# Index scores over 128 rows in both passes, half of the modulation steps moved into the index loop, and the odd attention's mask as constant rows of queries and keys

## The chip, the cores and the metric

The kernel runs on one core of one Trainium2 chip. The metric is the device time of one execution in microseconds (us), the median of several runs. Five engines work side by side: PE (TensorE, matrix products), DVE (VectorE), ACT (ScalarE), POOL (GpSimd) and SP, whose queue issues nearly all DMAs here. Each works through its own instructions in order.

## The reference, cut to what matters

The reference is a two-layer encoder over 1024 positions of width 1024. Before each sub-layer the stream is modulated by six vectors made from a conditioning vector `c`. Layer 0 picks, for every query, 256 keys by an index score, and layer 1 has a latent attention with a chunk mask:

```python
cond = jax.nn.silu(c)
mod = (cond @ ada_w[l] + ada_b[l])[:, None, :]          # six parts of 1024
sh_m, sc_m, g_m, sh_f, sc_f, g_f = jnp.split(mod, 6, axis=-1)
...
limit = (qpos // 64 + 1) * 64                            # end of the query's own chunk
rel = relu(einsum('bthd,bsd->bths', q_idx, k_idx))       # 8 index heads of 64
score = einsum('bths,bth->bts', rel, w_scaled)           # then top 256 below the limit
...
logits = einsum('bthd,bshd->bhts', qh, kh) * scale       # layer 1: 64 + 32 rotary rows
logits = where(key_pos < limit, logits, NEG); p = softmax(logits)
```

## The kernel before

Everything lies transposed, with channels in the 128 partitions. A product in float32 accuracy is made of passes over a high and a low part: `mm3` (lines 286 to 291) issues three matmuls, at lines 288, 289 and 290.

**Index stage.** `index` (line 1528) runs over blocks of 128 queries from 7 down to 2, and in each over four index heads; it is called for heads 0 to 3 and then for heads 4 to 7, so 48 heads in all. `scores2` makes the scores of one head in chunks of up to 512 keys, each by two matmuls: line 1307 with all 128 rows of the head's query tile (64 rows hold the high part, the other 64 the low part) against `kih`, and line 1308 with the 64 high rows alone against `kil`. ACT takes the relu into `rl` (line 1537), and DVE adds it, weighted, to `dd` (lines 1540 and 1542). PE has two score buffers, and `rl` has two. After each head, 1.4 or 1.6 steps of the projections behind it are put into PE's order; a step is one `mm3` of 512 columns.

**Bisection.** The threshold of each query is found bit by bit, 31 bits from 30 down (lines 1680 to 1700). In a bit DVE proposes a candidate (`cand`, line 1618), ACT counts three blocks by their signs (line 1624), DVE counts three more (line 1576), and DVE decides (lines 1636 and 1637). Between counts and decision stands one `mods.step()`: one of 32 loads of 128x1024 modulation weights, and one DVE product with the conditioning row, summed along the row (line 377). Nine bits in ten also take one half projection, 24 matmuls of 512 columns; every second half projection has its weights divided, high on ACT (line 266) and low on DVE (line 267). DVE's and ACT's order here is that of the code, and PE's order is that of the code everywhere; elsewhere a scheduler orders DVE, ACT and POOL. Then come the exact threshold and the masks on DVE, and PE does what projections are left.

**Odd attention.** 64 units (8 heads, 8 query blocks each) go through a pipeline. `unit` (line 2027) makes scores from rows 0 to 95 of the query and key tiles, and then one matmul of one row and 64 columns (line 2033) adds the mask, a large negative number where the first 64 queries of a block meet the last 64 keys. Key tiles come from a ring of three, query tiles from a ring of two. Ahead of the pipeline stand the keys and queries of head 0 and eight products of values (`uv`), each copied out by ACT (`mv`, line 2067).

Of the kernel before, what the change touches and what calls it, by code (L numbers as in the profile page):

```python
# [10 lines left out]
F32 = mybir.dt.float32  # L11
F32R = mybir.dt.float32r
# [3 lines left out]
ALU = mybir.AluOpType  # L16
# [3 lines left out]
P = 128  # L20
D = 1024
S = 1024
# [12 lines left out]
NEGMASK = -float(2 ** 100)  # L35
# [37 lines left out]
def layout(inp):  # L73

    a = {}
# [95 lines left out]
    f = np.float32  # L171
# [24 lines left out]
    a["c_cnt"] = np.ascontiguousarray(  # L196
        np.broadcast_to((1.0 / cnt).astype(f).reshape(1, 64), (P, 64))
    )
    mk = np.zeros((1, 192), f)
    mk[0, :64] = 1.0  # L200
    mk[0, 128:] = NEGMASK
    a["c_mask"] = mk
    return a


# [1 line left out]
def trunk(ctx, tc, t, out):  # L207
    nc = tc.nc
    V, A, G, T = nc.vector, nc.scalar, nc.gpsimd, nc.tensor

    def pool(name, bufs=1, side="left", space=None):
        if space is not None:
            return tc.tile_pool(name=name, bufs=bufs, space=space, reuse_waits="tile")
        return tc.tile_pool(name=name, bufs=bufs, side=side, reuse_waits="tile")
# [27 lines left out]
    def load(dst, src, eng=None):  # L242
        (eng or nc.sync).dma_start(dst, src)
# [910 lines left out]
    class Unit:  # L1154
# [10 lines left out]
        def scores(self):  # L1165
            n = S if self.i >= 4 else HALF
            self.ps = self.psum.tile([P, n], F32, tag=f"s{n}", name="s", bufs=1)
            self.scores_fn(self.ps)
# [129 lines left out]
            A.copy(dst[n][own, c], src[own])  # L1298
            V.tensor_tensor(dst[n][rest, c], src[own], dst[n][own, c].bitcast(F32), ALU.subtract)

    def scores2(ps, i, q, kh, kl, rows):

        qc = slice(i * P, (i + 1) * P)
        w = (i + 1) * P
        for c in range(0, w, HALF):
            e = min(c + HALF, w)
            T.matmul(ps[:, c:e], lhsT=q[:, qc], rhs=kh[:, c:e], start=True, stop=False)
            T.matmul(ps[:, c:e], lhsT=q[rows, qc], rhs=kl[rows, c:e], start=False, stop=True)
            spend(2 * max(e - c, 256) / 2400.0)


# [15 lines left out]
    tmp = ipx.enter_context(pool("idxtmp", bufs=2, side="right"))  # L1327
    start = ExitStack()
    tmp0 = start.enter_context(pool("start", bufs=3))
    bias0 = bias_of(0, tmp0)  # L1330
    kih = ip.tile([P, S], F32R, name="kih")
    kil = ip.tile([P, S], F32R, name="kil")
    wiT = ip.tile([P, S], F32, name="wiT")
    wi = ip.tile([P, 8, 8], F32, name="wi")
    qi = ip.tile([P, 8, S], F32R, name="qi")
# [44 lines left out]
    for k in range(KD):  # L1380
# [22 lines left out]
    for hf in range(2):  # L1403
        c = half(hf)
        ps = first[0][2][:, c]
# [26 lines left out]
    ps = bank("wit")  # L1432
# [11 lines left out]
    class Projections:  # L1444
# [75 lines left out]
        def taps(self, m):  # L1520
            u, y = self.conv["u"], yb[:, m]
            A.mul(y, u[:, 0:S], ctap[:, m, 0:1])
            for k in (1, 2):
                V.scalar_tensor_tensor(
                    y, u[:, k : k + S], ctap[:, m, k : k + 1], y, ALU.mult, ALU.add
                )

    def index(heads, others, rate):
        n = 0.0
        for i in range(7, 1, -1):  # L1530
            w_ = (i + 1) * P
            for hd in heads:
                rows = slice(64 * (hd % 2), 64 * (hd % 2) + 64)
                ps = bank2("idx_s")
                scores2(ps, i, qi[:, hd], kih, kil, rows)
                rl = tmp.tile([P, S], F32, tag="rl", name="rl")
                A.activation(rl[:, :w_], ps[:, :w_], AF.Relu)
                wc = wi[:, i, hd : hd + 1]
                if hd == 0:
                    V.tensor_scalar(dd[i], rl[:, :w_], wc, None, ALU.mult)  # L1540
                else:
                    V.scalar_tensor_tensor(dd[i], rl[:, :w_], wc, dd[i], ALU.mult, ALU.add)
                n += rate
                while n >= 1.0:
                    next(others, None)
                    n -= 1.0
    products = Projections().steps()
    index(range(4), chain(more_queries(3), products), FILL[0])
    index(range(4, 8), products, FILL[1])
    ipx.close()  # L1550
    yb = evy.enter_context(pool("evyb")).tile([P, 4, S], F32, name="yb")
    evkv = ExitStack()
# [12 lines left out]
    tmp = prj.enter_context(pool("prj", bufs=1, side="right"))  # L1565
    sel = ExitStack()
    tk = sel.enter_context(pool("tk", side="right"))
    eq = tk.tile([P, S], F32, name="eq")
    pre = tk.tile([P, S], F32, name="pre")
    junk = [tk.tile([P, S], BF16, name=f"junk{e}") for e in "va"]  # L1570

    cond_row = bank2("cond_row")
    mods = Modulation(None, tk, 0, range(2, 6), D, 0, cond_row, (eq, pre))

    def count(cnt, d, w, thr, op):
        V.tensor_scalar(junk[0][:, :w], d, thr, 0.0, op, ALU.add, accum_out=cnt)
# [105 lines left out]
    with tc.manual_schedule(engines={E.DVE}):  # L1682
        rows_ = Rows()
        rows_.setup()
        with tc.manual_schedule(engines={E.Activation}):
            pace = 0.0
            for bit in range(30, -1, -1):
                rows_.propose(bit)
                rows_.signs()
                rows_.counts()  # L1690
                mods.step()
                pace += PACE
                if pace >= 1.0:
                    advance()
                    pace -= 1.0
                rows_.decide()
            advance()
            mods.step()
        for nm, src in (("q", q32), ("k", k32)):
            split(*pairs[0, nm], src[:, 0])  # L1700
        rows_.step_up()
        rows_.result()
        rows_.mask()
# [10 lines left out]
    with ExitStack() as s:  # L1714
        pp = s.enter_context(pool("pair", bufs=2, side="right"))
# [107 lines left out]
    odp = od.enter_context(pool("od"))  # L1823
# [5 lines left out]
    load(pws, t["pool_s"])  # L1829
    latg = odp.tile([P, 5], F32, name="latg")  # L1830
    load(latg, t["lat_g"])
    mask = odp.tile([1, 192], F32R, name="mask")
    ones_lat = odp.tile([P, 2, P], F32, name="ones_lat")
    V.memset(ones_lat[:, 0], 1.0 / 384)
    V.memset(ones_lat[:, 1], 1.0 / 256)
# [14 lines left out]

    with ExitStack() as s:
        tmp = s.enter_context(pool("odprj", bufs=1))
        mraw = tmp.tile([1, 192], F32, tag="pu", name="mraw")
        load(mraw, t["c_mask"])
        V.tensor_copy(mask, mraw)
        edge = tmp.tile([P, 4, 16], F32, name="edge")
        V.memset(edge, 0.0)

# [102 lines left out]
    with ExitStack() as s:  # L1961
# [5 lines left out]
        v32 = vp.tile([P, 8, HALF], F32, name="mv32")  # L1967
        kk_, qq_, vv_ = {}, {}, {}

        def prepare_k(m):  # L1970
            kh = [pp.tile([P, S], F32R, tag="kh", name="kh", bufs=3) for _ in range(2)]
            kl = [pp.tile([P, S], F32R, tag="kl", name="kl", bufs=3) for _ in range(2)]
            for e in range(2):
                kk_[2 * m + e] = (kh[e], kl[e])
            raw = fetch(t["w_uk"][m], f"uk{m}")
            yield
            yield
            w = divide(raw, t["w_uk"].shape[-1], f"uk{m}", "pool")
            yield
            for e in range(2):  # L1980
                split(kh[e][64:96], kl[e][64:96], kr[64:96], lo_eng="pool")
            for hf in range(2):
                c = half(hf)
                ps = bank("uk")
                project(ps, w, P, [(a[:, c], b[:, c]) for a, b in kvx])
                yield
                for e in range(2):
                    split(kh[e][0:64, c], kl[e][0:64, c], ps[64 * e : 64 * e + 64])
                    if e == 0:
                        yield  # L1990

        def prepare_q(hd):
            raw = fetch(t["w_uq"][hd], f"uq{hd}")
            qh = pp.tile([P, S], F32R, tag="qh", name="qh")
            ql = pp.tile([P, S], F32R, tag="ql", name="ql")
            qq_[hd] = (qh, ql)
            yield
            yield
            w = divide(raw, t["w_uq"].shape[-1], f"uq{hd}", "pool")
            yield  # L2000
            qts = []
            for hf in range(2):
                c = half(hf)
                ps = bank("uq")
                project(ps, w, P, [(lat[:, 0, k, c], lat[:, 1, k, c]) for k in range(3)])
                yield
                qt = tmp.tile([P, HALF], F32, tag="q32", name="qt")
                A.mul(qt[0:64], ps[0:64], 96 ** -0.5)
                rotate(qt[64:96], ps, 64, 64, c, tmp, "rq1", "rq2")
                qts.append((c, qt))  # L2010
            yield
            for c, qt in qts:
                split(qh[0:96, c], ql[0:96, c], qt[0:96], lo_eng="pool")
                yield
# [10 lines left out]
                pass  # L2025

        def unit(hd, i, first):
            w_ = (i + 1) * P
            m, n = hd // 2, hd % 2

            def sc(ps):
                scores(ps, i, qq_[hd], kk_[hd], slice(0, 96))
                T.matmul(
                    ps[:, w_ - 64 : w_], lhsT=mask[:, 0:128], rhs=mask[:, 128:192],
                    start=False, stop=True, skip_group_check=True,
                )

            def peak(ps, pr, mx):
                V.tensor_reduce(mx, ps, AX.X, ALU.max, negate=True)

# [12 lines left out]

            return Unit(tmp, psum, (2,2), i, first, sc, peak, weigh, lambda: vv_[hd], put, store)
# [92 lines left out]
```

## Time and profile before

| | us |
|---|---|
| median of 3 runs (2680.07 to 2691.18) | 2689.89 |
| profiled execution, device time | 2674.74 |
| span of the profiled execution, first to last instruction | 2672.9 |
| index stage, first score matmul to last `dd` | 82.7 to 199.9 |
| bisection, first candidate to last decision | 211.2 to 388.5 |
| exact threshold and masks on DVE | 388.5 to 459 |
| odd attention, first score on PE to last | 1633.2 to 1843 |

A view by stretches gives each engine's busy time in it; the timeline gives single instructions, with the idle time ahead of them in brackets and what ended it. PEclk 1.00 stands for 2.4 GHz and 0.50 for 1.2 GHz. A matmul's stated duration overlaps the next one, so its price is read from start to start.

### The profile page before, as it was taken

To read this page: it belongs to the slowest core of one execution; us is meant where nothing else is said; L and a number is where in the kernel's file an instruction comes from. 1 tells how busy PE (TensorE), PEld (TensorE's weight loads), DVE (VectorE), ACT (ScalarE), POOL (GpSimd) and SP (SyncE) were. 2 spreads that over 40 slices of the span, in tenths; PEclk is the share of its full clock that TensorE was granted. 3 is DMA by queue.
4 is the path that set the end of the run, shared out by engine and by line. 5 is a ranking of instruction groups with operands and counts; after the bars stand their busy time and mean duration, and the time that the engine had idled before them with its cause. 6 is when DMAs were issued, how large, how long until landed. Compare 5 with 4: busy or idle time off the path is not lost. (4 is left out here: it accounts for less than half of the span.)

```text
span 2672.9 us, 32638 instructions
## 1 busy us (share of the span) xinstructions
PE 2467.4 (92%) x10922; PEld 1936.7 (72%) x10922; DVE 2157.8 (81%) x3491; ACT 1364.8 (51%) x2427; POOL 1054.5 (39%) x800
## 2 busy tenths in 40 slices
PE   6999998999888989998999899999888999998997
PEld 5567776887666767786777677787666888877786
DVE  6549899777698999978887866877698877788977
ACT  3446751765554444554333546766464555563434
POOL 0000001645674222424547634643865333334546
PEclk9899999999989989999999999999989999999999
DMA  6004430013434555335323331123533322244313
GB/s 244 32 18 136 139 118 16 17 68 120 129 104 153 183 173 166 126 98 178 91 75 95 105 101 61 54 75 106 173 100 103 107 86 84 95 128 148 102 47 105
DMA packets 123690, 284.43 MB, mean 106 GB/s; under 512 B 15361, under 2 KB 23042, under 8 KB 122626
## 3 DMA queue, kind: packets, MB, share of 16 engines
q1 hardware_dynamic: 122370, 278.16, 32.8%
q10 hardware_dynamic: 1152, 4.19, 0.4%
q8 instruction: 86, 1.41, 0.2%
q14 instruction: 82, 0.67, 0.1%
HBM read 234.06 MB, written 48.23 MB: 106 GB/s over the span
## 5 line engine op out<-in xcount | busy, mean ns | idle before, releaser
L702 DVE SCALAR_TENSOR_TENSOR cv<-u,taps,cv 128x512 f32<-128x512 f32 x352 | 311.1, 910 | 19.1 <-ACT cv L700 17.5
L267 POOL TENSOR_TENSOR v<-v,v 128x512 fp32r<-128x512 f32 x8 | 12.6, 1580 | 443.6 <-ACT v L266 443.6
L998 DVE SCALAR_TENSOR_TENSOR r<-dn,mod,r 128x512 f32<-128x512 f32 x198 | 147.0, 745 | 44.4 <-PE dn L290 42.5
L833 POOL TENSOR_TENSOR s<-rawg 128x512 f32<-128x512 f32 (+3 forms) x60 | 79.4, 1323 | 256.4 <-DVE wlo_ups L267 87.3
L700 ACT ACTIVATE cv<-u,taps 128x512 f32<-128x512 f32 x176 | 124.3, 721 | 58.0 <-DMA z<-cv 32.8
L288 PE MATMUL up<-t,wh 128*128 128x512 f32 x288 | 119.5, 415 | 33.1 <-ACT u L872 33.1
L706 ACT ACTIVATE cv<-cv 128x512 f32<-128x512 f32 x88 | 55.6, 632 | 144.7 <-DVE cv L702 143.9
L289 PE MATMUL up<-h_f,whi_up 128*128 128x512 f32 x256 | 105.5, 412 | 24.8 <-DVE h_f L267 24.8
L872 ACT COPY u<-up 128x512 f32<-128x512 f32 x144 | 83.9, 583 | 75.8 <-issue 35.3
L267 DVE TENSOR_TENSOR wl<-rawg,wh 128x512 fp32r<-128x512 f32 (+3 forms) x120 | 116.1, 970 | 2.6 <-ACT wh L266 2.4
L289 PE MATMUL up<-t,wh 128*128 128x512 f32 x288 | 117.7, 409 | 0.0
L290 PE MATMUL up<-t,wl 128*128 128x512 f32 x288 | 117.3, 407 | 0.0
L288 PE MATMUL up<-h_f,whi_upa 128*128 128x512 f32 x288 | 114.6, 398 | 1.2 <-ACT whi_upa L266 1.2
L834 POOL TENSOR_TENSOR s<-s,raw_upv 128x512 f32<-128x512 f32 x36 | 51.4, 1428 | 161.9 <-DMA raw_upv<-in_w_up 145.7
L266 ACT CAST wh<-rawg 128x512 fp32r<-128x512 f32 (+3 forms) x120 | 65.0, 545 | 97.6 <-PE dn L289 52.4
L290 PE MATMUL up<-h_f,wlo_upa 128*128 128x512 f32 x288 | 113.7, 395 | 0.7 <-DVE wlo_upa L267 0.7
L267 DVE TENSOR_TENSOR pl<-pt,ph 128x128 fp32r<-128x128 f32 (+2 forms) x192 | 99.4, 546 | 18.3 <-ACT ph L266 18.1
L266 ACT CAST ph<-pt 128x128 fp32r<-128x128 f32 (+2 forms) x192 | 85.3, 480 | 54.6 <-PE pt L1197 53.1
L289 PE MATMUL up<-h_f,whi_upa 128*128 128x512 f32 x288 | 113.0, 392 | 0.0
L290 PE MATMUL up<-h_f,wlo_up 128*128 128x512 f32 x256 | 104.6, 409 | 6.0 <-POOL wlo_up L267 6.0
L288 PE MATMUL up<-h_f,whi_up 128*128 128x512 f32 x256 | 106.4, 416 | 2.9 <-ACT h_f L266 1.9
L1624 ACT ACTIVATE junka<-dd,cand 128x384 bf16<-128x384 f32 (+2 forms) x93 | 87.1, 936 | 39.9 <-DVE cand L1618 37.9
(750 smaller groups left out, 8617.3 us busy)
## 6 DMA issues: line engine op xcount, KB each, us to landing
mod_raw<-in_ada_w SPq DMA_DIRECT2D x96, 256.0 KB, 2.9
z<-cv SPq DMA_DIRECT2D x88, 256.0 KB, 2.0
raw_upv<-in_w_up SPq DMA_DIRECT2D x36, 512.0 KB, 3.7
rawg<-in_w_up SPq DMA_DIRECT2D x34, 512.0 KB, 3.7
raw_up<-in_w_up SPq DMA_DIRECT2D x32, 512.0 KB, 3.7
z<-z SPq DMA_DIRECT2D x56, 256.0 KB, 2.9
xa_dram<-xo SPq DMA_DIRECT2D x48, 256.0 KB, 2.1
raw_dr<-in_w_dr SPq DMA_DIRECT2D x32, 384.0 KB, 3.1
```

Of the source, the lines that this page charges most:

```text
L266: A.copy(hi, src)
L267: (V if lo_eng == "dve" else G).tensor_tensor(lo, src, hi.bitcast(F32), ALU.subtract)
L288: T.matmul(ps, lhsT=wh, rhs=xh, start=start, stop=False, skip_group_check=more)
L289: T.matmul(ps, lhsT=wh, rhs=xl, start=False, stop=False, skip_group_check=more)
L290: T.matmul(ps, lhsT=wl, rhs=xh, start=False, stop=stop, skip_group_check=more)
L700: A.activation(y[n], u[:, 0:HALF], AF.Copy, scale=self.taps[:, c, 0:1])
L702: V.scalar_tensor_tensor(y[n], u[:, k : k + HALF], self.taps[:, c, k : k + 1], y[n], ALU.mult, ALU.add,)
L706: A.activation(y[1], y[1], AF.Silu)
L833: G.tensor_tensor(s1, g[:, c0], g[:, c1], ALU.add)
L872: A.copy(dst, ps)
L998: V.scalar_tensor_tensor(r, ps, self.gate[:, dt : dt + 1], r, ALU.mult, ALU.add)
L1624: A.activation(junk[1][:, :w], d, AF.Sign, bias=self.col(self.cand.bitcast(F32), j), scale=-1.0, accum_out=self.col(self.cnt, j),)
```

## The change

In `scores2` the second pass runs over all 128 rows too. `Modulation` is made twice: parts 2 and 3 (16 steps) with their own buffers inside `index`, a step after every even head of blocks 7 to 3 until 16 are done, and parts 4 and 5 in the bisection, on odd bits and once behind them. In the odd attention the query and key tiles are fixed, two and three pairs, rows 96 to 127 of each are filled once from a table, and the mask matmul goes.

```diff
+    mk = np.zeros((32, 2, 8, 2, 64), f)
+    mk[np.arange(8), 0, np.arange(8), 0] = 1.0
+    mk[np.arange(8), 1, np.arange(8), 1] = NEGMASK
+    a["c_mask"] = mk.reshape(32, 2 * S)
...
-            T.matmul(ps[:, c:e], lhsT=q[rows, qc], rhs=kl[rows, c:e], start=False, stop=True)
+            T.matmul(ps[:, c:e], lhsT=q[:, qc], rhs=kl[:, c:e], start=False, stop=True)
...
+    modx = ExitStack()
+    modp = modx.enter_context(pool("modp"))
+    mods = Modulation(modp, modp, 0, range(2, 4), D, 3)
...
-                scores2(ps, i, qi[:, hd], kih, kil, rows)
+                scores2(ps, i, qi[:, hd], kih, kil)
+                if i > 2 and hd % 2 == 0:
+                    mods.step()
...
-    mods = Modulation(None, tk, 0, range(2, 6), D, 0, cond_row, (eq, pre))
+    mods = Modulation(None, tk, 0, range(4, 6), D, 0, cond_row, (eq, pre))
...
-                mods.step()
+                if bit % 2:
+                    mods.step()
...
+        for n, tiles in enumerate((qtile, ktile)):
+            raw = tmp.tile([P, S], F32, tag="prb", name="mask_raw", bufs=2)
+            load(raw[96:], t["c_mask"][:, n * S : (n + 1) * S])
+            for hi, lo in tiles:
+                A.copy(hi[96:], raw[96:])
+                V.tensor_tensor(lo[96:], raw[96:], hi[96:].bitcast(F32), ALU.subtract)
...
-                scores(ps, i, qq_[hd], kk_[hd], slice(0, 96))
-                T.matmul(
-                    ps[:, w_ - 64 : w_], lhsT=mask[:, 0:128], rhs=mask[:, 128:192],
-                    start=False, stop=True, skip_group_check=True,
-                )
+                scores(ps, i, qq_[hd], kk_[hd], slice(0, P))
```

On DVE, at the start of the index stage, this stood before: `wi` are the head weights, `dd_98` and `dd_97` (`dd7` below) the scores of blocks 7 and 6, and `qi` the rest of the queries.

```order
L1435 COPY wi<-wit 128x64
L1540 TENSOR_SCALAR dd_98<-rl,wi 128x1024
L1542 SCALAR_TENSOR_TENSOR dd_98<-rl,wi,dd_98 128x1024 x3
L1540 TENSOR_SCALAR dd_97<-rl,wi 128x896
L1542 SCALAR_TENSOR_TENSOR dd_97<-rl,wi,dd_97 128x896
L1299 TENSOR_TENSOR qi<-qi 64x512
```

And now from the same copy on (lines are those of the changed kernel; `mod_raw` is a modulation step, whose row sum is the row behind it):

```order
L1436 COPY wi_126<-wit_633 128x64
L378 ISA mod_raw_721,mod_acc_660<-mod_raw_721,cond_row0_652 128x1024
L378 ISA mod_acc_660 128x1
L1547 TENSOR_SCALAR dd7_98<-rl_664,wi_126 128x1024
L378 ISA mod_raw_753,mod_acc_660<-mod_raw_753,cond_row0_652 128x1024
```

The scheduler does not leave the steps behind every second head: two stand ahead of this copy, and all 16 stand before the tenth of the 48 `dd` instructions, with the last casts of `qi` among them.

On PE, the first two units of the odd attention stood so, with the mask matmul at the end of each:

```order
L288 MATMUL s<-kh,qh 128x128
L289 MATMUL s<-kl,qh 128x128
L290 MATMUL s<-kh,ql 128x128
L2033 MATMUL s<-mask 128x64
L288 MATMUL s<-kh,qh 128x512
L289 MATMUL s<-kl,qh 128x512
```

Now the same two units run into each other:

```order
L289 MATMUL s<-kh_12953,qh_12959 128x128
L290 MATMUL s<-kl_12954,qh_12959 128x128
L291 MATMUL s<-kh_12953,ql_12960 128x128
L289 MATMUL s<-kh_12953,qh_12959 128x512
L290 MATMUL s<-kl_12954,qh_12959 128x512
```

64 mask matmuls are gone, and nothing stands in their place.

On ACT, ahead of that pipeline, the copies of the value products (`mv`) were broken only by the query casts. Now five fills of the constant rows stand behind the first of them:

```order
L2024 ACTIVATE qt<-uq 64x512 x2
L2078 COPY mv_12952<-uv 128x512
L1985 CAST qh_12959<-mask_raw 32x1024
L1985 CAST qh_12961<-mask_raw 32x1024
L1985 CAST kh_12953<-mask_raw 32x1024
L1985 CAST kh_12955<-mask_raw 32x1024
L1985 CAST kh_12957<-mask_raw 32x1024
L2078 COPY mv_12952<-uv 128x512
L267 CAST qh_12959<-qt 96x512
```

The seven later copies and both query casts moved behind the fills; five matching DVE instructions stand among the rotations of the first queries.

## Rows read from the trace of the kernel before

**Rows 1.** Stretches: length, then busy time of each engine, clock, DMA share, GB/s.

```profile
82.00:200.00 118.00, 117.86 (x377) 69.33 (x378) 50.67 (x58) 46.06 (x63) 0.00 (x0) 0.94 0.04 14
211.00:389.00 178.00, 168.06 (x719) 133.41 (x718) 161.32 (x382) 128.81 (x235) 0.00 (x0) 0.98 0.45 134
389.00:459.00 70.00, 61.83 (x266) 49.49 (x264) 68.08 (x101) 9.56 (x11) 4.38 (x2) 0.97 0.09 30
1633.00:1855.00 222.00, 212.49 (x1233) 175.17 (x1232) 169.17 (x332) 149.67 (x347) 108.42 (x113) 0.99 0.18 53
```

**Rows 2.** Timeline of PE, one index head: start, duration, line, tile, shape.

```profile
150.61 0.40 PE L1307 MATMUL idx_s<-kih,qi 128*128 128x512 f32 x1
150.94 0.50 PE L1308 MATMUL idx_s<-kil,qi 64*128 64x512 f32 x1
151.37 0.50 PE L1307 MATMUL idx_s<-kih,qi 128*128 128x512 f32 x1
151.80 0.49 PE L1308 MATMUL idx_s<-kil,qi 64*128 64x512 f32 x1
152.23 0.50 PE L288 MATMUL q<-h_m,whi_('q', 1)_884 128*128 128x512 f32 x1
152.56 0.40 PE L289 MATMUL q<-h_m,whi_('q', 1)_884 128*128 128x512 f32 x1
152.80 0.40 PE L290 MATMUL q<-h_m,wlo_('q', 1)_885 128*128 128x512 f32 x1
```

**Rows 3.** The tile `idx_s`: its 64-row matmuls, with shapes and counts.

```profile
L1308 PE MATMUL idx_s<-kil,qi x80: 323/491/793, 83.4 to 198.3; 64*128 64x512 f32 x48, 64*128 64x384 f32 x16, 64*128 64x256 f32 x8, 64*128 64x128 f32 x8
```

**Rows 4.** Stretches: the first of the index stage.

```profile
82.00:92.00 10.00, 9.86 (x20) 5.09 (x20) 2.82 (x5) 2.13 (x3) 0.00 (x0) 0.50 0.00 0
```

**Rows 5.** Timeline of DVE: the tenth head's `dd`.

```profile
114.04 1.02 DVE L1542 SCALAR_TENSOR_TENSOR dd<-rl,wi,dd 128x768 f32<-128x768 f32 x1 [1.55 <-ACT rl L1537]
```

**Rows 6.** Timeline of DVE: two bits of the bisection.

```profile
277.56 0.17 DVE L1618 TENSOR_TENSOR cand<-small,bits 128x6 int32<-128x6 int32 x1
...
280.41 1.22 DVE L377 CUSTOM_DVE_ANT_0 eq<-eq,cond_row 128x1024 f32<-128x1024 f32 x1
...
281.55 0.16 DVE L1636 TENSOR_TENSOR small<-cnt,small 128x6 int32<-128x6 f32 x1
...
281.95 0.17 DVE L1618 TENSOR_TENSOR cand<-small,bits 128x6 int32<-128x6 int32 x1
...
286.34 1.22 DVE L267 TENSOR_TENSOR wlo_('v', 3)_1938<-raw_('v', 3)_1848,whi_('v', 3)_1937 128x1024 fp32r<-128x1024 f32 x1 [0.31 <-ACT whi_('v', 3)_1937 L266]
...
287.88 0.17 DVE L1618 TENSOR_TENSOR cand<-small,bits 128x6 int32<-128x6 int32 x1
```

**Rows 7.** Timeline of ACT: the cast behind the second of these bits' signs.

```profile
285.27 1.03 ACT L266 CAST whi_('v', 3)_1937<-raw_('v', 3)_1848 128x1024 fp32r<-128x1024 f32 x1
```

**Rows 8.** DMA issues in the bisection: count, size, median us to landing.

```profile
pre<-in_ada_w SPq DMA_DIRECT2D x16, 512.0 KB, 3.7
```

**Rows 9.** Timeline of PE behind a wait in the bisection.

```profile
281.49 0.80 PE L288 MATMUL v<-h_m,whi_('v', 2)_1844 128*128 128x512 f32 x1 [2.65 <-ACT v L1518]
282.08 0.63 PE L289 MATMUL v<-h_m,whi_('v', 2)_1844 128*128 128x512 f32 x1
282.50 0.63 PE L290 MATMUL v<-h_m,wlo_('v', 2)_1845 128*128 128x512 f32 x1
```

**Rows 10.** Timeline of PE: the end of one unit of the odd attention.

```profile
1765.01 0.28 PE L289 MATMUL s<-kl,qh 96*128 96x256 f32 x1
1765.13 0.28 PE L290 MATMUL s<-kh,ql 96*128 96x256 f32 x1
1765.34 0.29 PE L2033 MATMUL s<-mask 1*128 1x64 f32 x1
1765.56 0.55 PE L1197 MATMUL pt<-ident,prs 128*128 128x128 f32 x3
```

**Rows 11.** Timeline of ACT ahead of the odd attention: two casts of 32 rows.

```profile
1613.45 1.99 ACT L266 CAST kh<-kr 32x1024 fp32r<-32x1024 f32 x2 [1.78 <-DVE kr L1849]
```

More of the change, by code (lines that the diff above doesn't have):

```diff
@@ L198, in layout @@
     )
[L199 to L202, printed above, removed]
+    mk = np.zeros((32, 2, 8, 2, 64), f)
+    mk[np.arange(8), 0, np.arange(8), 0] = 1.0
+    mk[np.arange(8), 1, np.arange(8), 1] = NEGMASK
+    a["c_mask"] = mk.reshape(32, 2 * S)
     return a
@@ L1299, in stack, with scores2 @@
             V.tensor_tensor(dst[n][rest, c], src[own], dst[n][own, c].bitcast(F32), ALU.subtract)
-    def scores2(ps, i, q, kh, kl, rows):
+    def scores2(ps, i, q, kh, kl):
         qc = slice(i * P, (i + 1) * P)
@@ L1532, in index @@
             for hd in heads:
-                rows = slice(64 * (hd % 2), 64 * (hd % 2) + 64)
                 ps = bank2("idx_s")
-                scores2(ps, i, qi[:, hd], kih, kil, rows)
+                scores2(ps, i, qi[:, hd], kih, kil)
+                if i > 2 and hd % 2 == 0:
+                    mods.step()
                 rl = tmp.tile([P, S], F32, tag="rl", name="rl")
@@ L1549, in trunk @@
     index(range(4, 8), products, FILL[1])
+    modx.close()
     ipx.close()
@@ L1831, in trunk @@
     load(latg, t["lat_g"])
-    mask = odp.tile([1, 192], F32R, name="mask")
     ones_lat = odp.tile([P, 2, P], F32, name="ones_lat")
@@ L1852, in trunk @@
         tmp = s.enter_context(pool("odprj", bufs=1))
-        mraw = tmp.tile([1, 192], F32, tag="pu", name="mraw")
-        load(mraw, t["c_mask"])
-        V.tensor_copy(mask, mraw)
         edge = tmp.tile([P, 4, 16], F32, name="edge")
@@ L1968, in trunk @@
         kk_, qq_, vv_ = {}, {}, {}
+        ktile, qtile = (
+            [[pp.tile([P, S], F32R, name=f"{nm}{e}{n}", bufs=1) for e in "hl"] for n in range(b)]
+            for nm, b in (("k", 3), ("q", 2))
+        )
+        for n, tiles in enumerate((qtile, ktile)):
[4 more added lines that the diff above has]
+                V.tensor_tensor(lo[96:], raw[96:], hi[96:].bitcast(F32), ALU.subtract)
         def prepare_k(m):
-            kh = [pp.tile([P, S], F32R, tag="kh", name="kh", bufs=3) for _ in range(2)]
-            kl = [pp.tile([P, S], F32R, tag="kl", name="kl", bufs=3) for _ in range(2)]
+            tiles = [ktile[(2 * m + e) % 3] for e in range(2)]
+            kh, kl = zip(*tiles)
             for e in range(2):
-                kk_[2 * m + e] = (kh[e], kl[e])
+                kk_[2 * m + e] = tiles[e]
             raw = fetch(t["w_uk"][m], f"uk{m}")
@@ L1993, in prepare_q @@
             raw = fetch(t["w_uq"][hd], f"uq{hd}")
-            qh = pp.tile([P, S], F32R, tag="qh", name="qh")
-            ql = pp.tile([P, S], F32R, tag="ql", name="ql")
-            qq_[hd] = (qh, ql)
+            qh, ql = qq_[hd] = qtile[hd % 2]
             yield
@@ L2027, in unit @@
         def unit(hd, i, first):
-            w_ = (i + 1) * P
             m, n = hd // 2, hd % 2
             def sc(ps):
-                scores(ps, i, qq_[hd], kk_[hd], slice(0, 96))
-                T.matmul(
-                    ps[:, w_ - 64 : w_], lhsT=mask[:, 0:128], rhs=mask[:, 128:192],
-                    start=False, stop=True, skip_group_check=True,
-                )
+                scores(ps, i, qq_[hd], kk_[hd], slice(0, P))
             def peak(ps, pr, mx):
```

## The prediction

> **What bounds the kernel now.** I read the view by stretches first, since the change touches three of them [rows 1]. In the index stage PE is busy for 117.9 of 118 us and DVE for 50.7, so what PE does there sets its length. In the bisection DVE is busy for 161 of 178 us and PE for 168, so neither can shrink far alone. Behind it DVE is busy for 68 of 70 us and PE for 62: the threshold and mask instructions on DVE set the end, and PE has 8 us to spare. In the odd attention PE is busy for 212 of 222 us, DVE for 169 and ACT for 150. Then I read the timelines at the places of the change.
>
> **The second index pass.** In one head at full clock [rows 2] the 64-row matmul at 150.94 starts 0.33 us behind the 128-row one, and then 0.43 us pass from start to start at every change between 64 and 128 rows; behind the last change the next matmul still takes 0.33 (152.23 to 152.56). Where 128 rows follow 128 rows it is 0.24 (152.56 to 152.80; 0.234 in the mean of longer runs). So the five gaps from 150.61 to 152.56 take 1.95 us where five plain ones take 5 x 0.234 = 1.17: 0.78 us more for two 64-row passes, 0.39 each. There are 80 such passes [rows 3]: 80 x 0.39 = 31 us of PE time; the shorter chunks pay the same, since it is paid per change.
>
> A check: 160 score matmuls have 2 x (48x512 + 16x384 + 8x256 + 8x128) = 67,584 columns [rows 3], the other 217 of the 377 [rows 1] have 512 each. At 0.234 us per 512 that is 30.9 + 50.8 = 82 us. 118 less 82 is 36: 31 are the changes, some 5 the start at half clock [rows 4].
>
> No 64-row pass runs beside another one in these rows: each starts 0.43 us from its neighbours [rows 2]. The Trainium skill, page "TensorE: Matmul & The Clock Gate", Part 3 (packing small matmuls), says that matmuls on different row groups of the array run concurrently, which speaks against filling all rows. By it, passes of an even and an odd head share a slot, the change adds 9 us in place of taking 31, and the sum below ends near no change; the trace does not agree, since no two such passes follow each other. I go by the rows.
>
> **The modulation steps in the index stage.** All 16 stand on DVE ahead of the tenth head's `dd`. A step takes 1.14 us to the next instruction's start (280.41 to 281.55) [rows 6], so 16 take 18. The first ten `dd` take about 10 (1.02 us for 768 columns [rows 5]; four have 1024, three are plain products and cost less), two query casts 1.4, small ones 1. That is 31 us from about 83.5, so the tenth `dd` ends near 115, as it does now (114.04 + 1.02) [rows 5]. PE has two score buffers and ACT two `rl`, so in these ten heads PE waits for DVE, and their 20 passes save nothing. The other 60 save 60 x 0.39 = 23 us; DVE has there only what it has now. The conditioning row's silu on ACT (about 1.0 us by the 1024 columns of [rows 7]) stands ahead of the last query casts and delays the first score by less than 1 us. I take **-22 us**. The loads: three buffers, 3.7 us from issue to landing [rows 8], so three steps per 3.7 + 1.14 + 0.4 us, 1.75 us a step against the 31/16 = 1.9 of DVE: hidden, barely. Thirteen of them also stand in SP's queue ahead of the weights of the keys, but PE comes to the keys only behind the index stage. Bounds: if no head waits for DVE, 31 less 1, -30; if a load took 7 us, three steps would take 8.5 and 16 of them 45, 14 more, -8.
>
> **The bisection.** 16 of the 31 bits lose their step. A bit without a division takes 4.39 us (277.56 to 281.95), one with a division 5.93 (281.95 to 287.88) [rows 6]. In the latter DVE waits 0.31 us for ACT's cast, which starts at 285.27, 3.3 us behind the candidate, when the signs are through [rows 7]: ACT sets that bit, and a missing step gives nothing. A plain bit falls to where the signs end plus the decision (281.55 to 281.95), 3.3 + 0.1 + 0.4 = 3.8 to 3.9, so by 0.5 and not by 1.14. By the code's order ten of the 16 are plain, five are divided, one is the last: 10 x 0.5 = 5 us. PE limits it too: a half projection is 24 x 0.234 = 5.6 us, 0.9 of it per bit is 5.05, against 178/31 = 5.74 per bit now. I take **-4**, bounds 0 (PE holds every bit) and -10 (178 less PE's 168). DVE's chain behind stays at 70 us and moves with it; PE's 8 us to spare there [rows 1] cover that, and without them PE's last projections would end later than the masks.
>
> **The odd attention.** From the last score to the mask matmul 0.21 us pass, and 0.22 from the mask to the next [rows 10]. Plain 256 columns take 0.12 (1765.01 to 1765.13), what 128 rows take at 0.234 per 512, so the step from 96 to 128 rows costs nothing. The mask costs 0.09 + 0.22 = 0.31 us, and 64 units make 20 us of PE. With 20 less PE has 192 us of work where DVE has 169 and ACT 150 [rows 1], so some of it becomes waits: 0.8 x 20 = **-16**, bounds -8 and -21.
>
> **The fills.** Two casts of 32 rows take 1.99 us on ACT [rows 11], so five take 5, and they stand behind the first copy of a value product. A product is 6 x 0.234 = 1.4 us, with four buffers. Counted from the first one's start, copy 1 ends at 2.0, the fills at 7.0 and copy 2 at 7.6; the sixth product, which needs copy 2's buffer, would start at 7.0. So the first score moves by **+1 us**. DVE's five, 1.2 us each by the 1024 columns of [rows 6], fit into its wait for the first score. If the two table loads, queued behind weights, land 4 us later than the first copy, it is +5; below 0 is excluded, since nothing leaves that place but a cast of one row.
>
> **Sum.** -22 - 4 - 16 + 1 = -41 us. The profiled execution took 2674.74 us (1.8 more than its span), so one like it would take 2634. It lies 15 us below the median of the runs shown, 2689.89; for a median I forecast 2689.9 - 41 = 2649 us. About 0.5%, 13 us, is what a measurement of this kernel can tell from no change.
>
> **The rivals.**
> - *Loads set the pace of the first heads.* The steps wait on DVE for weights, and every `dd` behind them too. For it: 1.75 against 1.9 us is no margin. Against: at 14 GB/s little else moves there [rows 1]. At 7 us a load the index stage saves 8, the sum is -27: 2663 us.
> - *The odd attention becomes bound by DVE and ACT.* For it: DVE would be busy for 169 of some 205 us, in a pipeline in which every unit passes four engines. Against: PE waits there for only 10 us of 222 now. At -8 the sum is -33: 2657 us.
> - *PE stays at 1.2 GHz through the index stage, and the kernel gets slower.* For it: behind a wait of 2.65 us a matmul takes 0.42 us (282.08 to 282.50) [rows 9], the stage begins at 0.50 now [rows 4], and DVE will make PE wait in each of ten heads. If the clock did not come back, 82 us of columns would take 82 x 0.42/0.234 = 147, 29 more than the 118 of now: +29 - 4 - 16 + 1 = +10, 2700 us. The change loses from 137 us on, that is when over 80% of the stage runs at half clock. Against: the stage begins so now, and its mean is 0.94 [rows 1]; from the eleventh head on DVE has half its time free.
> - *The 64-row pass was cheap.* If an even head's pass ran beside an odd head's, a pass would cost half of 0.234 and the change would add 80 x 0.117 = 9 us: +9 - 4 - 16 + 1 = -10, 2680 us, within what counts as the same. Against: the 0.43 us of [rows 2].
> - *The change does not do what it says*: fixed tiles could order the writes for the next head behind more reads than the rings did. The rings of three and two wait for the same readers, so I expect no price.
>
> **How the numbers follow.** My forecast 0.64; loads 0.14; attention bound 0.14; half clock 0.03; cheap pass 0.02; the last and others 0.03. The likeliest gives 2649. The bounds sum to -30 - 10 - 21 + 0 = -61 (2629) and -8 + 0 - 8 + 5 = -11 (2679). The upper end wants every term at its worst, so I take 2672, which holds both rivals on that side; the lower end gets 3 us, since the runs shown spread over 11: 2626 to 2672. Faster by over 0.5%: 0.64 + 0.14 + 0.14 = 0.92; slower: half clock and a third of the others, 0.04; the same: cheap pass and the rest, 0.04.
>
> **What would show it.** Index stage: score matmuls 0.234 us apart whatever the pass, the tenth `dd` at about 115, the last at about 178 instead of 199.9, steps on DVE with no long wait for a DMA. Bisection: plain bits without a step at 3.9 us, divided ones still at 5.9. Odd attention: no 0.2 us gap behind the scores, first to last score some 16 us shorter. The forecast is wrong if PE's clock is at 0.50 past 120 us, if steps wait for loads by over 5 us in all, or if PE's waits for ACT and DVE in the odd attention grow by more than 10.

## The result and the profile after

The changed kernel takes 2643.02 us (median of 4 runs, 2637.21 to 2646.66) where the kernel before, run beside it, takes 2687.86: a ratio of 0.9835, 95% interval 0.9807 to 0.9864. In a second comparison it took 2640.64 us, ratio 0.9843 (0.9819 to 0.9868). The forecast was 2649, its range 2626 to 2672. The profiled execution took 2637.21 us.

The head of its page: busy time, share of the span and count of instructions of each engine.

```profile
span 2635.4 us, 32516 instructions
PE 2415.2 (92%) x10858; PEld 1928.7 (73%) x10858; DVE 2167.5 (82%) x3495; ACT 1370.0 (52%) x2433; POOL 1057.3 (40%) x800
```

PE lost 52 us of busy time and the span 37.5. Where they went is read from the same events in both timelines (us, before and after; the shift is how much earlier an event comes than it did):

| event | before | after | shift |
|---|---|---|---|
| first index score on PE | 82.7 | 83.3 | -0.6 |
| last `dd` of the index stage ends | 199.9 | 175.0 | 24.9 |
| first candidate of the bisection | 211.2 | 186.2 | 25.0 |
| last decision | 388.3 | 353.4 | 34.9 |
| masks done, first peak of the even attention | 459.4 | 429.5 | 29.9 |
| first `uk` of the odd attention | 1613.3 | 1581.8 | 31.5 |
| first score of the odd attention | 1633.2 | 1602.2 | 31.0 |
| last score of the odd attention | 1842.8 | 1801.0 | 41.8 |
| end of the span | 2672.9 | 2635.4 | 37.5 |

Three stages gain (25, 10 and 11 us), and two give some back: 5 us between the last decision and the masks, and 4 behind the odd attention, where the change touches nothing. The other 1.6 us lie between the masks and the first `uk`.

The stretches of the changed kernel, in the columns of [rows 1]: the index stage in three pieces, the bisection, the threshold and masks, the odd attention from first to last score.

```profile
83.20:86.30 3.10, 3.10 (x9) 2.50 (x9) 3.04 (x6) 0.91 (x1) 0.00 (x0) 0.51 0.63 174
86.30:114.90 28.60, 22.08 (x99) 17.16 (x99) 26.95 (x43) 11.79 (x15) 0.00 (x0) 1.00 0.68 220
114.90:175.00 60.10, 59.22 (x270) 48.30 (x269) 37.82 (x45) 32.96 (x47) 0.00 (x0) 1.00 0.10 28
186.00:354.00 168.00, 163.29 (x708) 131.00 (x707) 143.09 (x347) 128.20 (x234) 0.00 (x0) 0.99 0.31 92
353.50:429.50 76.00, 64.51 (x278) 51.62 (x276) 69.48 (x103) 10.13 (x12) 3.51 (x2) 0.94 0.09 28
1602.20:1801.00 198.80, 182.84 (x1101) 157.45 (x1099) 162.96 (x319) 143.68 (x334) 108.11 (x113) 0.98 0.20 58
```

And the kernel before, its index stage cut at full clock and behind the tenth `dd`, then its odd attention:

```profile
82.60:96.50 13.90, 13.90 (x26) 7.33 (x26) 3.74 (x5) 3.07 (x3) 0.00 (x0) 0.50 0.00 0
96.50:115.10 18.60, 18.60 (x60) 10.24 (x59) 8.44 (x9) 7.49 (x9) 0.00 (x0) 1.00 0.00 0
115.10:199.90 84.80, 84.80 (x290) 51.24 (x291) 37.86 (x43) 35.32 (x50) 0.00 (x0) 1.00 0.06 20
1633.20:1842.80 209.60, 202.28 (x1164) 166.44 (x1162) 161.58 (x316) 143.13 (x332) 106.14 (x111) 0.99 0.18 55
```

The changed kernel has full clock 3 us behind the first score, the kernel before 14 us behind it. In the second row of the changed kernel DVE is busy for 27 of 28.6 us and PE for 22: those are the ten heads with the modulation steps among them. In the third PE has hardly a gap. In the fifth DVE, the engine that sets this stretch, has 6.5 us without work where it had 2 in [rows 1]. In the last PE is idle for 16 us.

**The index stage.** PE's timeline, to be read against [rows 2]:

```profile
149.96 0.40 PE L291 MATMUL q<-h_m,wlo_('q', 1)_924 128*128 128x512 f32 x1
150.19 0.39 PE L1308 MATMUL idx_s<-kih,qi 128*128 128x512 f32 x1
150.42 0.40 PE L1309 MATMUL idx_s<-kil,qi 128*128 128x512 f32 x1
150.66 0.28 PE L1308 MATMUL idx_s<-kih,qi 128*128 128x256 f32 x1
```

Score to score is 0.23 us now, as between the matmuls of a projection; the 0.33 and 0.43 are gone. The Trainium skill, page "TensorEngine Tiling (Array Packing)", section Key Properties, says that a change of the tiling mode drains TensorE; the 0.43 us of [rows 2] against the 0.23 here agree. On DVE the tenth `dd`, with the last modulation step ahead of it:

```profile
112.74 1.23 DVE L378 CUSTOM_DVE_ANT_0 mod_raw<-mod_raw,cond_row 128x1024 f32<-128x1024 f32 x1 [0.29 <-DMA mod_raw<-in_ada_w]
113.89 1.02 DVE L1549 SCALAR_TENSOR_TENSOR dd<-rl,wi,dd 128x768 f32<-128x768 f32 x1
```

It ends at 114.9, as it did before [rows 5], and the wait of 0.29 us for a load is one of four, 1.6 us in all.

**The bisection.** One bit without a step and without a division, in the columns of [rows 6]:

```profile
205.74 0.17 DVE L1626 TENSOR_TENSOR cand<-small,bits 128x6 int32<-128x6 int32 x1
...
209.13 0.17 DVE L1644 TENSOR_TENSOR small<-cnt,small 128x6 int32<-128x6 f32 x1 [0.45 <-ACT junka L1632]
...
209.54 0.17 DVE L1626 TENSOR_TENSOR cand<-small,bits 128x6 int32<-128x6 int32 x1
```

It takes 3.80 us, and DVE waits for ACT's signs at its end. The bit behind it, which is divided, takes 5.93 as before (209.54 to 215.47).

Behind the bisection DVE waits for what PE's projections release: for their results (`xb`), and for weights that ACT casts only when PE has let go of the buffer. First its waits in the changed kernel from 353.4 to 429.5, then all that it had before from 388.4 to 459.4 (us in all, times, longest):

```profile
DVE cx L1507 <- PE xb L291: 2.4, 3, 1.2
DVE wlo_('cg', 3)_2863 L268 <- ACT whi_('cg', 3)_2862 L267: 2.4, 1, 2.4
DVE wlo_('bg', 3)_2983 L268 <- ACT whi_('bg', 3)_2982 L267: 0.2, 1, 0.2
```

```profile
DVE cx L1506 <- PE xb L290: 0.3, 1, 0.3
```

**The odd attention.** PE's timeline at the end of a unit, against [rows 10], and PE's waits from first to last score:

```profile
1701.71 0.28 PE L290 MATMUL s<-kl,qh 128*128 128x256 f32 x1
1701.83 0.28 PE L291 MATMUL s<-kh,ql 128*128 128x256 f32 x1
1701.95 0.49 PE L1198 MATMUL pt<-ident,prs 128*128 128x128 f32 x3
```

```profile
PE s L289 <- ACT prb L2053: 6.4, 7, 1.7
PE s L289 <- ACT prs L2053: 4.4, 5, 1.5
PE pt L1198 <- DVE pl L268: 2.1, 1, 2.1
PE yps L1235 <- DVE pl L268: 2.1, 2, 1.8
```

And PE's waits before, in the same stretch:

```profile
PE s L288 <- ACT prs L2042: 3.0, 4, 1.1
PE s L288 <- ACT prb L2042: 2.0, 5, 0.7
PE yps L1234 <- DVE pl L267: 1.0, 1, 1.0
PE pt L1197 <- DVE pl L267: 1.0, 1, 1.0
```

The last score is followed by the transpose 0.12 us later; 0.43 passed before. With short waits for `kl`, which are not shown, the waits sum to 15.5 us now and to 7.2 before. Most are scores that wait until the exponentials have read the score buffer.

**The fills** on ACT, behind the first copy of a value product:

```profile
1591.83 0.59 ACT L2078 COPY mv<-uv 128x512 f32<-128x512 f32 x1 [0.82 <-PE uv L291]
1592.44 1.99 ACT L1985 CAST qh<-mask_raw 32x1024 fp32r<-32x1024 f32 x2
1594.34 2.93 ACT L1985 CAST kh<-mask_raw 32x1024 fp32r<-32x1024 f32 x3
1597.30 0.59 ACT L2078 COPY mv<-uv 128x512 f32<-128x512 f32 x1
```

They take 4.9 us. The value products on PE stretch from 11.0 us, first to last, to 11.8.

### The profile page after: what moved, and what is told of

It reads as the page before. It is cut to its first block, busy times and chain, and to the rows that moved or that the text cites. A ratio compares the mean times of both kernels' runs of the same rounds, so it can differ in the third digit from the quotient of the medians.

```text
span 2635.4 us, 32516 instructions
## 1 busy us (share of the span) xinstructions
PE 2415.2 (92%) x10858; PEld 1928.7 (73%) x10858; DVE 2167.5 (82%) x3495; ACT 1370.0 (52%) x2433; POOL 1057.3 (40%) x800
## 5 line engine op out<-in xcount | busy, mean ns | idle before, releaser
L999 DVE SCALAR_TENSOR_TENSOR r<-dn,mod,r 128x512 f32<-128x512 f32 x198 | 147.1, 745 | 40.8 <-PE dn L291 39.3
L378 DVE CUSTOM_DVE_ANT_0 mod_raw<-mod_raw,cond_row 128x512 f32<-128x512 f32 (+1 forms) x112 | 105.9, 951 | 18.4 <-DMA mod_raw<-in_ada_w 14.7
L289 PE MATMUL up<-h_f,whi_upa 128*128 128x512 f32 x288 | 114.5, 398 | 1.2 <-ACT whi_upa L267 1.2
L268 DVE TENSOR_TENSOR pl<-pt,ph 128x128 fp32r<-128x128 f32 (+2 forms) x192 | 99.5, 546 | 16.7 <-ACT ph L267 16.1
```

Source lines behind the costliest of these rows:

```text
L268: (V if lo_eng == "dve" else G).tensor_tensor(lo, src, hi.bitcast(F32), ALU.subtract)
L289: T.matmul(ps, lhsT=wh, rhs=xh, start=start, stop=False, skip_group_check=more)
L378: V.tensor_tensor_reduce(out=raw, in0=raw, in1=self.cond[:, o], scale=1.0, scalar=0.0, op0=ALU.mult, op1=ALU.add, accum_out=self.acc[:, j, ...
L999: V.scalar_tensor_tensor(r, ps, self.gate[:, dt : dt + 1], r, ALU.mult, ALU.add)
```

## The experiments

The theory: a change between 64 and 128 rows costs PE 0.39 us per index pass; the moved steps are paid for in the first ten heads and in waits of the threshold instructions for PE; the mask matmuls' 20 us are half turned into waits for ACT and DVE. The rivals: the pass was cheap and the steps made the gain, or the odd attention lost its gain for another reason. Times with a ratio to the kernel before on the same chip (2682 to 2688 us).

**The pass alone** (kernel before, one line):

```diff
-            T.matmul(ps[:, c:e], lhsT=q[rows, qc], rhs=kl[rows, c:e], start=False, stop=True)
+            T.matmul(ps[:, c:e], lhsT=q[:, qc], rhs=kl[:, c:e], start=False, stop=True)
```

> The kernel before with the second index pass over 128 rows and nothing else. My theory: a change between 64 and 128 rows costs PE 0.39 us per pass, all 80 passes save it, so first score to last sum falls from 117 us to about 86, and the bisection and what follows are only moved: about 31 us in all, 2657 against 2688. If the 64-row passes are also what held the clock at 1.2 GHz until 96.5 us, full clock comes back by some 87 us and the stage ends at about 82, 36 us in all. Rival, that the 64-row pass was cheap and the gain in the changed kernel came from the moved steps: 5 to 10 us at most.

2645.99 us against 2683.37, ratio 0.9864 (0.9846 to 0.9882): 37 us, nearly all of the change's gain. First to last score takes 80.8 us (84.5 to 165.3), 115.6 before. Its stretches, clock in the third column from the right:

```profile
84.50:87.50 3.00, 3.00 (x8) 2.38 (x8) 0.36 (x2) 0.89 (x1) 0.00 (x0) 0.53 0.00 0
87.50:165.30 77.80, 77.80 (x360) 64.66 (x359) 48.60 (x54) 43.74 (x60) 0.00 (x0) 1.00 0.07 21
```

PE has no gap, and full clock is there after 3 us; before, it came after 14. The rival of a cheap pass falls. The rule of the Trainium skill that stood for it (page "TensorE: Matmul & The Clock Gate", Part 3) is not tested by this: no run here put 64-row passes on different rows side by side.

**The move alone** (kernel before; `Modulation` of parts 2 and 3 inside `index`, the rest on odd bits, 64-row passes kept):

```diff
                 scores2(ps, i, qi[:, hd], kih, kil, rows)
+                if i > 2 and hd % 2 == 0:
+                    mods.step()
```

> The kernel before with half of the modulation steps moved into the index loop and nothing else. My theory: PE is so slow with its 64-row passes that DVE's 18 us of steps fit beside them, the tenth sum still ends near 115 us and the index stage grows by no more than 2 us; the bisection shrinks by 10 us as in the changed kernel (177 to 167), and 5 of them come back as waits of the threshold instructions for PE's projections. Net 4 to 6 us faster, about 2683. Rival, that the steps hold up the index stage: it grows by 8 us or more and the whole is slower by 3 or more.

2685.72 us, ratio 1.0005 (0.9993 to 1.0018): nothing, where 4 to 6 us were expected. The tenth `dd` ends at 126.4 us and not near 115, since PE stays at half clock until 119.9 us, where the profile before has full clock from 96.5:

```profile
83.10:119.00 35.90, 35.90 (x66) 18.92 (x66) 23.41 (x37) 8.82 (x10) 0.00 (x0) 0.50 0.53 162
```

The fair comparison is with the next kernel, which has no steps there and a stretch of half clock as long: first to last score takes 125.4 us here and 125.3 there, so the steps do not make the stage longer. The bisection takes 167.0 us, 177.1 before. But from the last decision to the first product of values in the even attention 91.6 us pass where 84.9 did: the waits for PE give back 7 of the 10. The two that grew most:

```profile
DVE wlo_('cg', 3)_2863 L267 <- ACT whi_('cg', 3)_2862 L266: 4.0, 1, 4.0
DVE cx L1506 <- PE xb L290: 2.4, 3, 1.2
```

From the first index score to the first product of values 396.9 us pass, against 397.5 in the next kernel. So here too the move is worth next to nothing.

**The constant rows alone** (kernel before, with the last two pieces of the change's diff):

```diff
-                scores(ps, i, qq_[hd], kk_[hd], slice(0, 96))
-                T.matmul(
-                    ps[:, w_ - 64 : w_], lhsT=mask[:, 0:128], rhs=mask[:, 128:192],
...
+                scores(ps, i, qq_[hd], kk_[hd], slice(0, P))
```

> The kernel before with the constant mask rows and without the mask matmuls, nothing else. My theory: PE's work in the odd attention falls by 64 x 0.31 = 20 us, PE's waits for DVE and ACT grow by about 8 us, and first score to last score falls from 209 us to 198 or 199, 10 to 12 us in all: about 2677. Rival 1, that the loss in the changed kernel came from something else that was changed earlier: it falls by 16 to 20. Rival 2, that the price of a mask matmul is far below 0.31: PE's busy time there falls by less than 10 us.

2674.25 us, ratio 0.9965 (0.9951 to 0.998): 9 us. First to last score takes 201.3 us, in the columns of [rows 1]:

```profile
1642.60:1843.90 201.30, 185.63 (x1100) 159.66 (x1099) 162.77 (x318) 143.64 (x334) 107.97 (x113) 0.97 0.19 57
```

PE's busy time falls by 16.7 us and its waits are those of the changed kernel to 0.3 us, so the loss belongs to this part. That the busy time falls by 2.7 us less than in the changed kernel goes with the clock: 14 us of this stage are at 1.2 GHz, 7 in the changed kernel and 3 in the kernel before. This profile also shows the half clock in an index stage that is the kernel before's to the letter:

```profile
82.20:115.00 32.80, 32.80 (x59) 16.87 (x59) 9.36 (x11) 8.01 (x9) 0.00 (x0) 0.50 0.00 0
```

PE works without a gap and stays at 1.2 GHz until 118.7 us.

**64-row passes back in the first ten heads** (changed kernel):

```diff
+                early = hd < 4 and 4 * (7 - i) + hd < 10
+                rows = slice(64 * (hd % 2), 64 * (hd % 2) + 64) if early else slice(0, P)
+                scores2(ps, i, qi[:, hd], kih, kil, rows)
```

> The changed kernel, with the 64-row second pass again in the first ten index heads alone (20 of 80 passes). My theory: DVE sets the pace of these heads, so PE's wait of some 7 us in them shrinks or goes, the tenth sum still ends at about 115 us (within 1) and the kernel's time stays at 2643 within 4. If the half clock until 96.5 us in the kernel before went with 64-row passes, it is back here too, well past 86 us, and the tenth sum may then come up to 3 us later. Rival, that these ten heads had gained as the others did: 8 us slower, 2651, the tenth sum near 123.

2646.8 us, ratio 0.987 (0.9852 to 0.9888). The median is within the 4 us, but by the ratio this kernel is 7 to 9 us slower than the changed one (0.9843 and 0.9835), near the rival's 8, though the intervals overlap. The profile speaks against the theory too: PE waits for nothing until 116 us, the tenth `dd` ends at 119.7, between the theory's 115 and the rival's 123, and first to last score takes 95.8 us instead of 90.2. The half clock is back until 96.0 us, for which the theory had allowed up to 3 us on the tenth `dd`:

```profile
82.60:96.00 13.40, 13.40 (x24) 6.95 (x24) 10.23 (x16) 3.07 (x3) 0.00 (x0) 0.50 0.74 232
```

The delay is 4.8. So these 20 passes are not free: with 64 rows, PE at half clock and not DVE sets the first of these heads. By their rows alone they would be nearly so: 20 x 0.39 = 7.8 us would almost fit into the 6.5 us that PE waits there in the changed kernel. It is the 10 us more at half clock, some 5 us of work, that seem to tip it; no run separates the two.

**Steps spread over the heads** (changed kernel):

```diff
+    with tc.manual_schedule(engines={mybir.EngineType.DVE}):
         index(range(4), chain(more_queries(3), products), FILL[0])
         index(range(4, 8), products, FILL[1])
```

> The changed kernel with DVE's instructions of the index loop in the order of the code, so that a modulation step stands behind every second or third head instead of 16 ahead of the tenth. My theory: bunched together, the steps make PE wait 7 us in the first ten heads; spread, they fit beside it. First score to last score falls from 90 us to 81 to 83, the bisection stays at 167, the waits of the threshold instructions for PE's projections shrink as PE is 7 us further, and the whole is 5 to 9 us faster than the changed kernel (ratio to before 0.980 to 0.982). Rival: DVE in the code's order waits for late scores or weights as long as it waited before, and the time stays within 3 us of the changed kernel.

2647.7 us, ratio 0.9861 (0.984 to 0.9883): no gain, and the question stays open, since the code's order brought a loss of its own. PE waited for the low parts of weights, and ACT for a load whose buffer came free late:

```profile
PE q L291 <- DVE wlo_q L268: 6.3, 1, 6.3
ACT whi_('q', 2)_1070 L267 <- DMA raw_('q', 2)_929<-in_w_ev: 9.0, 1, 9.0
```

The clock fell to 1.2 GHz once more while PE stood in the first of these waits, from 114.5 to 121.3 us.

**The change without the move** (all 32 steps in the bisection again):

```diff
-                if bit % 2:
-                    mods.step()
+                mods.step()
```

> The changed kernel with all 32 modulation steps in the bisection again, so the 128-row pass and the constant mask rows alone. My theory, from the kernels with one part each: the move takes 9 us in the index stage and 5 to 7 in the waits behind the bisection, and gives back 10 in the bisection, so without it the kernel is 3 to 6 us faster than the changed one: 2637 to 2640 where that has 2643, ratio to before 0.981 to 0.983. Rival: the move is worth its 10 us in the bisection, and without it the kernel is 4 us or more slower than the changed one.

2636.61 us, ratio 0.9826 (0.9805 to 0.9848); the changed kernel has 0.9835 and 0.9843. The median is 4 to 6 us lower, but the intervals overlap, so the time alone does not decide. The stages say where: first to last index score 81.4 us against 90.2, bisection 176.0 against 167.1, from there to the first values product 84.8 against 89.9, 5 less in the sum. It is not one profile's chance: from the first index score to that product the three kernels with 128-row passes and no move take 353.6 to 355.6 us, and four profiles with the move 359.4 to 362.3. In the changed kernel the move is a small loss.

**128 rows in the even attention too** (changed kernel; queries of a head in tiles with zeros in the other 64 rows, for three of four pairs):

```diff
-                lambda ps: scores(ps, i, pairs[m, "q"], pairs[m, "k"], rows),
+                lambda ps: scores(
+                    ps, i, qpad[n] if m else pairs[m, "q"], pairs[m, "k"],
+                    slice(0, P) if m else rows,
+                ),
```

> The changed kernel; in the even attention the queries of a head stand in tiles of their own with zeros in the other 64 rows, so that scores run over 128 rows there too, in 48 of the 64 units (the first pair of heads is left at 64 rows). My theory, that a change between 64 and 128 rows costs PE 0.1 us on the way in and 0.1 on the way out where 256 columns stand before it: 48 units give 8 to 12 us, since PE is busy for all of that stage, and the whole comes to 2632 to 2635. Rival: the split copies (four of 64 rows on ACT and on POOL where two of 128 stood) make these engines the bound, and less than 3 us is left.

2636.14 us, ratio 0.9829 (0.98 to 0.9857), 5 to 7 us below the changed kernel's two medians, but 2 to 4 by the ratios, with intervals that overlap. PE's timeline shows the price gone (0.12 us from the last score to the transpose, 0.21 with 64 rows):

```profile
500.06 0.28 PE L291 MATMUL s<-kh,ql 128*128 128x256 f32 x1
500.18 1.03 PE L1198 MATMUL pt<-ident,prb 128*128 128x128 f32 x8
```

From the first values product to the first matmul of the feed-forward part 223.7 us pass instead of 228.4; the ten profiles with 64 rows there have 228.4 to 231.9. Up to the last score of the stage it is 139.7 us against 147.1 to 148.0 in those ten, the 8 us expected. Three of them are lost behind it. What goes with that is the clock, 9 us at 1.2 GHz in the whole stretch where the changed kernel has 1, and longer waits of PE for casts by DVE and for POOL (2.2 and 2.8 us, 0.3 and 1.9 in the changed kernel).

**A third less score work in the odd attention** (changed kernel; the product of the queries' low with the keys' high part is left out of the computation):

```diff
-                scores(ps, i, qq_[hd], kk_[hd], slice(0, P))
+                    T.matmul(ps[:, c:e], lhsT=qq_[hd][0][:, qc], rhs=kk_[hd][0][:, c:e], start=True, stop=False)
+                    T.matmul(ps[:, c:e], lhsT=qq_[hd][0][:, qc], rhs=kk_[hd][1][:, c:e], start=False, stop=True)
```

> The changed kernel without the third pass of the scores in the odd attention (queries' low part by keys' high part), which is left out of the computation: PE has 17 us less work there (36,864 columns at 0.234 us per 512), and no other engine has less. My theory: after the change PE's slack is gone into waits for exponentials and casts, so of a further 17 us less than half shows, first score to last score falls from 199 us by 4 to 8, and PE's waits for ACT and DVE grow by 9 us or more. Rival: PE still sets the pace and the waits of the changed kernel have another cause; it falls by 14 to 17.

One run, 2638.9 us. First to last score 194.7 us, 4.1 less for 17 us of matmuls. PE's waits, of which two:

```profile
PE s L2050 <- ACT prb L2058: 8.4, 8, 2.0
PE s L2050 <- ACT prs L2058: 7.8, 9, 1.8
```

All of them sum to 21.8 us, 6.3 more and not the 9 expected. The mean clock fell from 0.98 to 0.96: 17 us of the stage are at 1.2 GHz, 7 in the changed kernel, which is some 5 us of work. So the gain has the size that the theory gave it, but waits are only one half of the reason and the clock is most of the other. The rival (14 to 17 us) falls: past the change, PE's work no longer sets this stage alone.

**The changed kernel again, and the parts that gained together** (without the move, with the padded queries).

> The changed kernel once more, beside the next one on the same chip. 0.9835 of the kernel before, within 0.003, that is 2639 to 2647 if that takes 2683 to 2688. Index stage 90 us from first to last score, bisection 167, odd attention 199 from first to last score.

> The 128-row pass and the constant mask rows with all modulation steps in the bisection, and the padded queries of the even attention: what gained, without what did not. If the parts add up, 3 to 6 us from leaving the move out and 5 to 7 from the even attention: 8 to 12 us faster than the changed kernel beside it, ratio to before 0.979 to 0.981. Rival: the even attention's gain was noise or is lost when its start moves, and it is within 4 us of the kernel without the move (ratio 0.982 to 0.983).

2640.64 us and 2628.05 us; ratios 0.9843 (0.9819 to 0.9868) and 0.9791 (0.9768 to 0.9813). The second is 12.6 us below the first, a little more than the 8 to 12 expected, with intervals that do not meet, and faster than both kernels of this case. Its even attention confirms the padded queries: 221.1 us from the first values product to the feed-forward part, 138.6 to the last score.

## Why the forecast was right, and which terms were off

Sum: -41 us were forecast, -45 and -42 measured in the two comparisons. What each part does to PE was foreseen; one step on the path behind it failed, and four terms were off by -3, -6, +5 and +5 us. That they cancel is luck, so the total says more for the forecast than its terms do. The terms below are read from one pair of profiles, which lie 37.5 us apart; the profile before is 13 us below its kernel's median of 2687.86. Where the medians differ by 4 to 7 us more is not shown.

- *The index stage, -22: it was -25.* In the profile before, 58 of the 80 passes come after the tenth `dd`: 58 x 0.39 = 22.6, the term as worked out. The rest is in "their 20 passes save nothing". PE did wait in these ten heads, 6.5 us, but with full clock from 86.3 us on, not 96.5, it still came out 20 matmuls further: 270 follow the tenth `dd` where 290 did, some 4 us. That 128 rows gain in these heads too was shown by putting 64 rows back (5.6 us longer), rows and clock together.
- *The bisection, -4: it was -10.* Plain bits fell to 3.80 to 3.87 us as forecast, divided ones stayed at 5.93, also three that lost their step, where DVE's wait for ACT's cast grew from 0.3 to 1.4 us: ACT sets those bits, as forecast. The 0.5 per bit was too little in the mean: three plain bits had taken 5.0, with one more DVE instruction, and fell by 1.15; and bits 15 and 14, where DVE had waited 2.1 and 2.5 us for ACT, whose copies waited for PE (3.8 and 1.9 us), fell by 1.9 and 0.9. Seven bits by 0.55, three by 1.15 and these two make 10. Not all of it is the steps': bit 15 keeps its step, and with the old bisection it took 4.60 to 6.82 us in five profiles, 4.88 in all with the new one. Over these the bisection takes 174.7 to 177.4 us and 167.0 to 167.3, so 7 to 10 is what the profiles show. The limit of PE at 5.05 us a bit did not bind: 167.1/31 is 5.4.
- *The chain behind, 0: it was +5.* "PE's 8 us to spare there [rows 1] cover that" is the step that failed. With the bisection 10 us shorter and PE's work the same, PE is busy without a gap through its last projection, until 416 us, and DVE waits 5.0 us for projections (0.3 before). The spare time lay at the end of the stretch, after PE's last projection, and not where DVE needs its results. The move alone shows the same: 10 us gained, 7 given back.
- *The odd attention, -16: it was -11.* PE's busy time fell by 19.4, as the 0.31 us per mask matmul said; its waits grew by 8.3 and ate two fifths, not one fifth. The rival of DVE and ACT, 8 us, came for 5 of them. The constant rows alone and the run with a third less score work show it; in the latter the clock has as large a part.
- *The fills, +1: +0.8*, the stretch of the value products.
- The remaining +4 at the end of the profile is the spread of executions: from the last odd score to the end 834 us pass here, 830 in the kernel before, 829 in the changed kernel's other profile, and 829 to 835 in all twelve.
- *Rivals.* Loads did not set the pace: 1.6 us of waits. Half clock did not persist; the change made it shorter. The fixed tiles cost nothing that shows, since the waits are for score buffers. None of the three signs of a wrong forecast came: full clock at 86.3 us and not past 120, 1.6 us of waits for loads and not 5, and 8.3 us more of waits in the odd attention, close to the 10.

## What to carry to other kernels

Price a matmul from start to start, not by its stated duration: one of 64 rows between two of 128 cost PE 0.39 us beyond its columns here, while three of 64 rows in a row cost 0.09 at their end (0.21 for 0.12 in the even attention). Filling the rows removed that from PE's timeline in all three places: with the product of the two low parts, which belongs to the exact sum, with the mask, or with zeros. Before work is moved off the engine that sets a stage, ask what that engine does next and which results it takes in the middle of it: spare time that the other engine had only behind its last result covered nothing here. And when a shared stage nears balance (PE 202, DVE 162, ACT 143 of 210 us), do not count on all that leaves its first engine: here 11 of 20 us showed, and then 4 of a further 17.

## What the runs showed of the hardware

The prediction did not expect the clock's recovery to depend on the passes. All twelve profiles begin the index stage at 1.2 GHz, behind a wait of PE of 2.3 to 4.6 us, with the first score at 81.1 to 84.5 us, and until full clock comes PE works without a gap in those shown above. By the granted clock, the four with 64-row passes at the start were back at 2.4 GHz at 96.0, 96.5, 118.7 and 119.9 us, the eight with 128-row passes at 86.3 to 90.6. With or without the moved steps and their loads it is the same (96.5 and 118.7 without, 96.0 and 119.9 with), and two pairs of kernels differ in the passes alone: the kernel before and the pass alone (96.5 and 87.3), the 64-row passes put back and the changed kernel (96.0 and 86.3). So it goes with the passes; why is not shown. Why a stretch at half clock lasted 14 us in one execution and 37 in another with the same passes stays open too. It fits that the pass alone gave 37 us where the change of rows accounts for 31: 11 us less at half clock are 5 us of work.
